# An encoder's two feed-forward layers: four form sums per layer on VectorE instead of GpSimd, and one more up chunk whose low parts a DMA makes

## The chip, the cores and the metric

The kernel runs on one core of one Trainium2 chip. The metric is device time in microseconds. Before the change the median of three runs was 1126.25 us (1124.7 to 1126.65).

## The reference

A small bidirectional encoder, batch 1, 512 tokens, width 1024, two residual layers in float32. Layer 0 mixes tokens by chunked gated linear attention, layer 1 by grouped-query attention. Each is followed by the feed-forward part that the change touches:

```python
def conv_ffn(h, w_up, w_conv, b_conv, w_down):
    u = h @ w_up                       # (512, 1024) @ (1024, 2*2816)
    u = lax.conv_general_dilated(      # depthwise, width 3, centred
        u, w_conv[:, None, :], window_strides=(1,), padding=[(1, 1)],
        dimension_numbers=('NWC', 'WIO', 'NWC'), feature_group_count=u.shape[-1]) + b_conv
    val, gate = jnp.split(u, 2, axis=-1)
    return (jax.nn.silu(gate) * val) @ w_down
...
x = x + conv_ffn(rmsnorm(x, norm_ffn[i]), ffn_w_up[i], ffn_w_conv[i], ffn_b_conv[i], ffn_w_down[i])
```

## The kernel before, in words

**High and low parts.** Every large product is made of three matmuls in a faster, less exact float format: each operand is split into a high part (the value rounded to that format) and a low part (what the rounding left). `mm3` issues high x high, high x low, low x high, so the third matmul of a product is the first that needs the weights' low part. In the names, `wh` and `wl` are the high and low parts of weights, `xhl` the two parts of the normalised input, `gu` those of the gated result, `raw` and `draw` the weights as they are loaded (up and down).

**Two kinds of up chunks.** The 5632 columns of the up matrix are taken in 22 chunks m of 128 value and 128 gate columns. The first six (`PLAIN`, m = 0 to 5) are plain: two halves (value, then gate) of 8 x 3 matmuls each over all 512 tokens into one PSUM bank `up`. The other 16 (`seven`) use a scheme of the Strassen kind with seven products of half-size blocks in place of eight; they need sums of weight blocks (`sum12`, `sum43`) and sums of blocks of the input, the *forms*. The forms are made once per layer, in `build()`, in small steps while the plain chunks run: eight `h` blocks, then the sums T1, T2, T3, T4 (tiles `ts`, line 740, by `combine`, two instructions of 128x512 for each), then a high and a low part of each form (`th`, line 734, ScalarE; `tl`, line 735, VectorE). T3 = B22 - B12 and T4 = T2 - B21 are summed on GpSimd. Chunk 6 is the first to read the forms.

**Where the low parts of the plain chunks' weights come from.** There are two ways. In `split` (lines 219 and 220) ScalarE copies the high part, rounding it, and VectorE subtracts it from `raw`. In `convert` with `by_dma` ScalarE copies the high part (line 166) and then a negative copy of `raw` into `wl` (line 168), and a DMA on GpSimd's queue adds `raw` to what is there (line 209, `accum_op=ALU.add`); the subtraction costs VectorE nothing. `BY_DMA` tells for how many plain chunks of each layer the second way is taken: 4, so chunks 0 to 3; chunks 4 and 5 are split.

**Buffers.** The parts of the weights lie in six buffers of 128x1024, that is three pairs: the next half's high copy can begin when TensorE has finished the half before the one it starts. `raw` has two buffers of a whole chunk (1 MB). A chunk's load waits until both low parts of the chunk two before it are made.

**After a plain chunk's half**: VectorE scales `up` by the token's norm into `u` (line 802), the convolution runs on ScalarE (775) and VectorE (776, 777), then silu (779), the product (780) and the split into `gu` (782, 783). Behind chunk 5 the first tiles of the down product follow (`dn`, `draw` weights, line 142 for the load, 166 and 171 for the parts), and then chunk 6 (`X`).

**What sets the order.** The functions are written in program order, but a scheduler sets each engine's order of instructions by its own costs and dependences. Each engine then works strictly in its order. An edit in one place can so move others; the change section shows where.

Of the kernel before, what the change touches and what calls it, by code (L numbers as in the profile page):

```python
# [13 lines left out]
ALU = mybir.AluOpType  # L14
# [29 lines left out]
AHEAD = 4  # L44
EARLY = 1
ROWS_AT = 3
BY_DMA = 4
FIRST_DMA = False
STEPS = 4
SHARES1 = (0, 2, 3, 3)  # L50
# [8 lines left out]
def hybrid_encoder_kernel(  # L59
# [21 lines left out]
    pe, act, dve, pool, sync = nc.tensor, nc.scalar, nc.vector, nc.gpsimd, nc.sync  # L81
# [25 lines left out]
    def big(dt, n):  # L107
        return pair("g", 22, dt, n)
# [147 lines left out]
    def add_ffn(layer):  # L256
        for m in range(PLAIN):
            W.todo.append((up[layer], m, 0))
            if m == PLAIN - 1:
                W.todo.append(("load", layer, PLAIN))  # L260
            W.todo.append((up[layer], m, 1))
            W.early += part_keys(layer, BESIDE[m])
            W.todo += part_keys(layer, BESIDE[m])
        for m in range(PLAIN, FC):
            if m + 1 < FC:
                W.todo.append(("load", layer, m + 1))
            W.todo += [(n, layer, m) for n in ("rowA1", "sum12", "sum43")]
            W.todo += part_keys(layer, BESIDE[m])
            W.todo.append(("oneA22", layer, m))
        W.todo += part_keys(layer, part_tiles(len(PARTS) - 1))  # L270
# [7 lines left out]
    add_ffn(1)  # L278
    W.by_dma += [(a, 1) for a in qk_order + [w_av]] + [(w_aout, 2)] + [(a, BY_DMA) for a in up]

# [427 lines left out]
    def ffn(layer, norm, cw, nxt):  # L708
# [4 lines left out]
        def build():  # L713

            hs = []
            for i in range(4):
                t = big(F32, "h")
                for e in range(2):
                    c = 2 * i + e
                    dve.scalar_tensor_tensor(t[:, e * S : (e + 1) * S], x[c], norm.weight(c), norm.R,  # L720
                                             ALU.mult, ALU.mult)
                    yield
                hs.append(t.rearrange("p (c s) -> p c s", s=S))
            q2 = (slice(0, 2), slice(2, 4))
            blk = lambda i, j: [hs[2 * i + q][:, :, j * H : (j + 1) * H] for q in range(2)]
            b11, b12, b21, b22 = blk(0, 0), blk(0, 1), blk(1, 0), blk(1, 1)
            v4 = lambda t: t.rearrange("p (k s) -> p k s", s=H)

            def pieces(name, srcs):
                hi, lo = v4(big(F32R, "th")), v4(big(F32R, "tl"))  # L730
                n = 4 // len(srcs)
                for q, src in enumerate(srcs):
                    sl = slice(q * n, (q + 1) * n)
                    act.activation(hi[:, sl], src, AF.Copy)
                    dve.tensor_tensor(lo[:, sl], src, hi[:, sl].bitcast(F32), ALU.subtract)
                forms[name] = (hi, lo)

            def combine(eng, dst, a, b, op):
                for q in range(2):
                    eng.tensor_tensor(dst[:, q2[q]], a[q], b[q], op)  # L740

            halves = lambda t: [t[:, q] for q in q2]
            pieces("B11", b11)
            yield
            t1, t2, t3 = (v4(big(F32, "ts")) for _ in range(3))
            combine(dve, t1, b11, b12, ALU.subtract)
            yield
            combine(dve, t2, b22, halves(t1), ALU.add)
            yield
            pieces("T2", [t2])  # L750
            yield
            pieces("T1", [t1])
            yield
            combine(pool, t3, b22, b12, ALU.subtract)
            combine(pool, t2, halves(t2), b21, ALU.subtract)
            yield
            pieces("B21", b21)
            yield
            pieces("B22", b22)
            yield  # L760
            pieces("T3", [t3])
            yield
            pieces("T4", [t2])
            yield

        building = build()

        def gated(m, u):
# [466 lines left out]
```

## Time and profile before

| | |
|---|---|
| profiled execution, time | 1126.34 us |
| its span | 1124.6 us |
| mean granted TensorE clock | 0.998 |
| TensorE, matmuls | 1104.3 us busy (98%) |
| VectorE | 887.7 us (79%) |
| ScalarE | 576.1 us (51%) |
| GpSimd | 121.2 us (11%) |
| low parts by accumulating DMA (line 209) | 32 DMAs of 512 KB, 5.3 us median from issue to landing |
| GpSimd's form sums (line 740) | 8 instructions, 20.0 us in all |
| plain chunks of layer 0 and 1 | about 232 to 300 us, about 764 to 833 us |

A row of the order of time reads: start, duration, engine, source line, operation, what is written from what, shapes, how many in a row, and in brackets how long the engine had been idle and which engine's instruction ended that. PE is TensorE, DVE VectorE, ACT ScalarE, POOL GpSimd, SP SyncE; a q behind a name is the engine's queue. Starts are microseconds from the start of the span. VectorE's and ScalarE's instructions overlap the next by some 0.1 us.

### The profile page before, as it was taken

What the parts mean: (1) busy time and instruction counts of PE and PEld (TensorE: products, weight loads), DVE (VectorE), ACT (ScalarE), POOL (GpSimd) and SP (SyncE); (2) the same over time, 40 slices, a digit from 0 to 9 for tenths busy, and PEclk for the clock granted to TensorE, in tenths of its full rate; (3) what the DMA queues carried; (4) which work ended last, traced back from release to release, by engine and by line L of the source; (5) the groups of instructions that cost most, each with busy time, mean ns of one, the idle gap of its engine ahead of it and who ended that gap; (6) DMA issues with size and microseconds to landing.
All of it is one profiled execution on the core that took longest, in us unless ns stands there. A gap on an engine that the chain in (4) does not pass through costs nothing.

```text
span 1124.6 us, 16137 instructions
## 1 busy us (share of the span) xinstructions
PE 1104.3 (98%) x6418; PEld 971.2 (86%) x6418; DVE 887.7 (79%) x1355; ACT 576.1 (51%) x854; POOL 121.2 (11%) x98
## 2 busy tenths in 40 slices
PE   9999999999899999999999999999999999999998
PEld 7878888888699999999978888888779999999996
DVE  6576654569989999979885588755997999997985
ACT  6455233465545455444474667646554545544441
POOL 0214210013000000000004333001400000000000
PEclk9999999999999999999999999999999999999999
DMA  6422220275332332323427755436433232332322
GB/s 218 142 97 76 75 75 27 97 161 128 132 112 95 112 96 93 118 73 110 168 50 195 187 159 160 140 105 159 122 131 113 95 112 83 105 113 76 113 75 75
DMA packets 30076, 128.64 MB, mean 114 GB/s; under 512 B 3505, under 2 KB 4145, under 8 KB 21297
## 3 DMA queue, kind: packets, MB, share of 16 engines
q1 hardware_dynamic: 20496, 102.30, 26.9%
q0 software_dynamic: 4608, 16.78, 7.8%
q10 hardware_dynamic: 4896, 8.54, 2.1%
q8 instruction: 50, 0.82, 0.3%
q14 instruction: 26, 0.20, 0.1%
HBM read 100.34 MB, written 2.10 MB: 91 GB/s over the span
## 4 chain that ended last, share of the span: by engine, by line
PE 78%; DVE 12%; issue 4%; ACT 3%; DMA 2%; POOL 1%; ACTq 0%; DVEq 0%; SPq 0%; POOLq 0%
PE dn L85 19%; PE Y L85 16%; PE X L85 12%; PE op L85 8%; PE vg L85 5%; PE k L85 2%; PE q L85 2%; PE up L85 2%; PE po L85 2%; PE s L85 2%; PE o L85 2%; PE A L85 1%; PE B L85 1%; DVE y L776 1%; DVE y L777 1%
## 5 line engine op out<-in xcount | busy, mean ns | idle before, releaser
L85 PE MATMUL dn<-gu,wh 128*128 128x512 f32 x708 | 219.8, 392 | 4.0 <-ACT wh L166 2.5
L85 PEld LDWEIGHTS dn<-gu,wh 128*128 128x128 f32 x708 | 130.9, 189 | 31.3 <-ACT wh L166 3.3
L85 PE MATMUL dn<-gu,wl 128*128 128x512 f32 x354 | 138.2, 391 | 1.6 <-DVE wl L171 1.6
L85 PE MATMUL up<-xhl,wh 128*128 128x512 f32 x384 | 118.8, 390 | 0.0
L775 ACT ACTIVATE y<-u,cw 128x512 f32<-128x512 f32 x88 | 68.0, 807 | 78.1 <-DVE u L875 64.1
L85 PE MATMUL X<-th,xwh 128*128 128x256 f32 x360 | 101.9, 283 | 0.0
L85 PE MATMUL X<-th,xwl 128*128 128x256 f32 x360 | 101.9, 283 | 0.0
L85 PE MATMUL X<-tl,xwh 128*128 128x256 f32 x360 | 101.9, 283 | 0.0
L166 ACT ACTIVATE wh<-raw 128x1024 fp32r<-128x1024 f32 x66 | 69.8, 1057 | 57.4 <-PE op L85 14.5
L841 DVE TENSOR_TENSOR x<-x,dn 128x512 f32<-128x512 f32 x95 | 64.7, 684 | 31.6 <-PE dn L85 31.4
L85 PEld LDWEIGHTS up<-xhl,wh 128*128 128x128 f32 x384 | 71.8, 188 | 14.8
L166 ACT ACTIVATE wh<-draw 128x1024 fp32r<-128x1024 f32 x44 | 46.7, 1061 | 71.9 <-PE dn L85 35.7
L85 PE MATMUL vg<-wh,xhl 128*128 128x512 f32 x256 | 80.3, 391 | 1.6 <-DVE wh L217 0.8
L209 POOL DMA_DIRECT2D wl<-raw x32 | 28.3, 883 | 493.1 <-ACT wl L168 487.9
L85 PEld LDWEIGHTS dn<-gu,wl 128*128 128x128 f32 x354 | 66.9, 189 | 16.0 <-DVE wl L171 2.2
L85 PE MATMUL up<-xhl,wl 128*128 128x512 f32 x192 | 75.0, 391 | 4.8 <-DVE wl L220 4.8
L85 PE MATMUL Y<-th,wh 128*128 128x256 f32 x264 | 74.7, 283 | 0.0
L85 PE MATMUL Y<-tl,wh 128*128 128x256 f32 x264 | 74.7, 283 | 0.0
L85 PE MATMUL Y<-th,wl 128*128 128x256 f32 x264 | 74.7, 283 | 0.0
L219 ACT ACTIVATE wh<-raw 128x1024 fp32r<-128x1024 f32 x40 | 42.0, 1053 | 59.9 <-PE op L85 18.8
L220 DVE TENSOR_TENSOR wl<-raw,wh 128x1024 fp32r<-128x1024 f32 x40 | 53.9, 1351 | 23.4 <-ACT wh L219 19.7
L85 PE MATMUL op<-oT,wh 128*128 128x512 f32 x256 | 71.1, 394 | 0.3 <-DVE oT L980 0.3
(232 smaller groups left out, 2872.4 us busy)
## 6 DMA issues: line engine op xcount, KB each, us to landing
raw<-in_w_up_dram SPq DMA_DIRECT2D x44, 1024.0 KB, 5.0
draw<-in_w_down_dram SPq DMA_DIRECT2D x44, 512.0 KB, 3.7
wl<-raw POOLq DMA_DIRECT2D x32, 512.0 KB, 5.3
pr<-p ACTq DMA_DIRECT2D x32, 256.0 KB, 2.5
raw<-in_w_vg_dram SPq DMA_DIRECT2D x6, 1024.0 KB, 5.0
raw<-in_w_akq_dram SPq DMA_DIRECT2D x5, 1024.0 KB, 6.2
raw<-in_w_kq_dram SPq DMA_DIRECT2D x4, 1024.0 KB, 4.8
raw<-in_w_gout_dram SPq DMA_DIRECT2D x4, 1024.0 KB, 5.1
```

The lines of the kernel that those rows point to most:

```text
L85: i = pe.matmul(*a, **k)
L166: act.activation(hi, r, AF.Copy)
L209: pool.dma_start(dst, src, accum_op=ALU.add)
L219: act.activation(hi[:, sl], r[:, sl], AF.Copy)
L220: dve.tensor_tensor(lo[:, sl], r[:, sl], hi[:, sl].bitcast(F32), ALU.subtract)
L775: act.activation(yt, ut, AF.Identity, scale=w(1), bias=w(3))
L776: dve.scalar_tensor_tensor(yt[:, 1:], ut[:, : S - 1], w(0), yt[:, 1:], ALU.mult, ALU.add)
L777: dve.scalar_tensor_tensor(yt[:, : S - 1], ut[:, 1:], w(2), yt[:, : S - 1], ALU.mult, ALU.add)
L841: dve.tensor_tensor(x[c], x[c], ps, ALU.add)
```

## The change

The two sums T3 and T4 go to VectorE, and `BY_DMA` becomes 5, so that chunk 4's weights get their low parts by DMA too, in both layers.

```diff
-BY_DMA = 4
+BY_DMA = 5
...
-            combine(pool, t3, b22, b12, ALU.subtract)
-            combine(pool, t2, halves(t2), b21, ALU.subtract)
+            combine(dve, t3, b22, b12, ALU.subtract)
+            combine(dve, t2, halves(t2), b21, ALU.subtract)
```

In the order of instructions this shows as follows. In layer 0, `raw_2149` is chunk 4's weights (`wh_2151`, `wl_2152` its first half), `raw_2232` (then `raw_2234`) chunk 5's; `ts_2072` to `ts_2074` are the form sums. GpSimd, before and after, from chunk 3's accumulates on:

```order
L209 DMA wl_2038<-raw_2035 128x1024
L209 DMA wl_2086<-raw_2035 128x1024
L740 TENSOR_TENSOR ts_2074<-h_2014,h_1977 128x512
L740 TENSOR_TENSOR ts_2074<-h_2017,h_1980 128x512
L740 TENSOR_TENSOR ts_2073<-ts_2073,h_2014 128x512
L740 TENSOR_TENSOR ts_2073<-ts_2073,h_2017 128x512
```
```order
L209 DMA wl_2038<-raw_2035 128x1024
L209 DMA wl_2086<-raw_2035 128x1024
L209 DMA wl_2152<-raw_2149 128x1024
L209 DMA wl_2191<-raw_2149 128x1024
L209 DMA wl_5032<-raw_5029 128x1024
```

The four sums have left the queue, and two accumulates of chunk 4 stand in their place. ScalarE, layer 0, from the high copy of chunk 4's first half on, before and after:

```order
L219 ACTIVATE wh_2151<-raw_2149 128x1024
L734 ACTIVATE th_2079<-ts_2073 128x1024
L775 ACTIVATE y_2135<-u_2033,cw 128x512
L734 ACTIVATE th_2114<-ts_2072 128x1024
L734 ACTIVATE th_2122<-h_2014 128x512
L734 ACTIVATE th_2122<-h_2017 128x512
L734 ACTIVATE th_2128<-h_2014 128x512
L734 ACTIVATE th_2128<-h_2017 128x512
L219 ACTIVATE wh_2189<-raw_2149 128x1024
```
```order
L166 ACTIVATE wh_2151<-raw_2149 128x1024
L734 ACTIVATE th_2079<-ts_2073 128x1024
L775 ACTIVATE y_2135<-u_2033,cw 128x512
L734 ACTIVATE th_2114<-ts_2072 128x1024
L168 ACTIVATE wl_2152<-raw_2149 128x1024
L734 ACTIVATE th_2122<-h_2014 128x512
L734 ACTIVATE th_2122<-h_2017 128x512
L166 ACTIVATE wh_2190<-raw_2149 128x1024
L168 ACTIVATE wl_2191<-raw_2149 128x1024
L734 ACTIVATE th_2128<-h_2014 128x512
L734 ACTIVATE th_2128<-h_2017 128x512
```

The negative copy of the first half (line 168) stands three instructions behind its high copy, and the second half's two copies have moved up between the form copies. In layer 1 the first half's negative copy stands directly behind its high copy. VectorE, layer 0, from the subtraction of chunk 4's first half on, before, and the same place after:

```order
L220 TENSOR_TENSOR wl_2152<-raw_2149,wh_2151 128x1024
L735 TENSOR_TENSOR tl_2080<-ts_2073,th_2079 128x1024
L735 TENSOR_TENSOR tl_2115<-ts_2072,th_2114 128x1024
L735 TENSOR_TENSOR tl_2123<-h_2014,th_2122 128x512
L735 TENSOR_TENSOR tl_2123<-h_2017,th_2122 128x512
```
```order
L735 TENSOR_TENSOR tl_2115<-ts_2072,th_2114 128x1024
L740 TENSOR_TENSOR ts_2074<-h_2014,h_1977 128x512
L740 TENSOR_TENSOR ts_2074<-h_2017,h_1980 128x512
L740 TENSOR_TENSOR ts_2073<-ts_2073,h_2014 128x512
L740 TENSOR_TENSOR ts_2073<-ts_2073,h_2017 128x512
L735 TENSOR_TENSOR tl_2123<-h_2014,th_2122 128x512
```

The subtraction is gone, and the four sums stand between the low parts of T1 and of B21. Some rows further down, the subtraction for chunk 5's first half stands ahead of the low parts of T3 and T4, where it stood behind them before.

## The prediction

> **What bounds the kernel now.** I read the page first, then TensorE's waits, then its order of time around each wait, and last VectorE (DVE), GpSimd (POOL), ScalarE (ACT) and the DMAs beside the longest ones.
>
> ```profile
> PE 1104.3 (98%) x6418; PEld 971.2 (86%) x6418; DVE 887.7 (79%) x1355; ACT 576.1 (51%) x854; POOL 121.2 (11%) x98
> ```
>
> TensorE is busy for 98% of the span, and the change takes no matmul away. All that can be won is idle time of TensorE, so its waits come next (engine, line and what it waited for: us in total, times, longest).
>
> ```profile
> PE up L85 <- DVE wl L220: 4.8, 2, 2.7
> PE dn L85 <- ACT wh L166: 2.5, 2, 1.8
> PE dn L85 <- DVE wl L171: 1.6, 1, 1.6
> PE X L85 <- ACT wh L166: 0.8, 1, 0.8
> ```
>
> These four rows are 9.7 us, and all of it lies in the plain chunks of the two FFN layers and directly behind them. Two are for low parts that VectorE makes (L220, L171). TensorE's order of time tells where (start, duration, then in brackets the idle time before and who ended it):
>
> ```profile
> 276.10 0.39 PE L85 MATMUL up<-xhl,wl 128*128 128x512 f32 x1
> ...
> 286.54 0.61 PE L85 MATMUL up<-xhl,wh 128*128 128x512 f32 x2
> 289.26 0.50 PE L85 MATMUL up<-xhl,wl 128*128 128x512 f32 x1 [2.10 <-DVE wl L220]
> ...
> 300.66 0.96 PE L85 MATMUL dn<-gu,wh 128*128 128x512 f32 x3 [0.66 <-ACT wh L166]
> 303.21 0.50 PE L85 MATMUL dn<-gu,wl 128*128 128x512 f32 x1 [1.59 <-DVE wl L171]
> ```
> ```profile
> 808.16 0.61 PE L85 MATMUL up<-xhl,wh 128*128 128x512 f32 x2
> 811.46 0.50 PE L85 MATMUL up<-xhl,wl 128*128 128x512 f32 x1 [2.69 <-DVE wl L220]
> ...
> 834.87 1.20 PE L85 MATMUL dn<-gu,wh 128*128 128x512 f32 x4 [1.81 <-ACT wh L166]
> ```
>
> A half of a chunk is 24 matmuls, and its third is the first that needs the low part. 276.10 is the third matmul of chunk 4's first half, 286.54 the first of chunk 5's: 46 matmuls in 10.44 us, 0.227 each. A matmul's modelled duration (0.39) overlaps the next one, so a bracket understates what is lost; I count start against due start. Chunk 5's third matmul was due at 286.54 + 2 x 0.227 = 286.99 and came at 289.26. Without any wait the down tile would start at 286.54 + 48 x 0.227 = 297.44, and its fourth matmul (first low part) at 298.12; it came at 303.21. So layer 0 loses 5.1 us here. In layer 1 chunk 4's third matmul was due at 808.16 + 0.45 = 808.61 and came at 811.46: 2.85 lost, and 1.8 more ahead of the down tile.
>
> Why is VectorE late? Line 740 is the sums of the input's forms, 776 and 777 the convolution:
>
> ```profile
> 262.86 4.42 DVE L740 TENSOR_TENSOR ts<-h 128x512 f32<-128x512 f32 x2
> 267.20 1.28 DVE L740 TENSOR_TENSOR ts<-h,ts 128x512 f32<-128x512 f32 x2
> ...
> 269.01 0.73 DVE L776 SCALAR_TENSOR_TENSOR y<-u,cw,y 128x511 f32<-128x511 f32 x1
> 269.67 1.21 DVE L220 TENSOR_TENSOR wl<-raw,wh 128x1024 fp32r<-128x1024 f32 x1
> ...
> 275.48 1.78 DVE L776 SCALAR_TENSOR_TENSOR y<-u,cw,y 128x511 f32<-128x511 f32 x1
> 277.18 2.43 DVE L777 SCALAR_TENSOR_TENSOR y<-u,cw,y 128x511 f32<-128x511 f32 x2
> ```
> ```profile
> 809.13 2.28 DVE L220 TENSOR_TENSOR wl<-raw,wh 128x1024 fp32r<-128x1024 f32 x1
> ```
> ```profile
> 263.86 2.86 POOL L740 TENSOR_TENSOR ts<-h,h 128x512 f32<-128x512 f32 x2
> 272.16 6.25 POOL L740 TENSOR_TENSOR ts<-ts,h 128x512 f32<-128x512 f32 x2 [5.44 <-DVE tl L735]
> ```
> ```profile
> 801.68 6.97 POOL L740 TENSOR_TENSOR ts<-ts,h 128x512 f32<-128x512 f32 x2 [6.19 <-DVE tl L735]
> 808.61 3.94 POOL L740 TENSOR_TENSOR ts<-h,h 128x512 f32<-128x512 f32 x2
> ```
>
> Just while GpSimd runs its sums, VectorE's instructions are stretched: two sums took 4.42 in place of 1.28, three convolution steps 1.78 + 2.43 = 4.21 in place of 3 x 0.73 = 2.19, and in layer 1 the very subtraction for which TensorE waits took 2.28 in place of 1.21. GpSimd holds VectorE up for 3.14 + 2.02 = 5.2 us in layer 0.
>
> **The change, part by part.** *Sums to VectorE.* Per layer VectorE gets four sums of 0.64 (1.28 for two), +2.6 us, and no longer stands beside GpSimd: -5.2 in layer 0. GpSimd loses its sums; nobody waited for them on TensorE's path.
>
> *Chunk 4's low parts by DMA.* VectorE loses two subtractions of 1.21: -2.4 per layer. So its line in layer 0 gets ahead by 5.2 + 2.4 - 2.6 = 5.0 us. ScalarE gets two negative copies, and GpSimd's queue two accumulating DMAs. ScalarE is strictly in order, so what counts is when each copy comes:
>
> ```profile
> 261.96 1.04 ACT L168 ACTIVATE wl<-raw 128x1024 fp32r<-128x1024 f32 x1
> ...
> 264.70 1.06 ACT L219 ACTIVATE wh<-raw 128x1024 fp32r<-128x1024 f32 x1 [0.98 <-PE up L85]
> 268.58 1.06 ACT L734 ACTIVATE th<-ts 128x1024 fp32r<-128x1024 f32 x1 [2.82 <-DVE ts L740]
> ...
> 271.20 2.18 ACT L734 ACTIVATE th<-h 128x512 fp32r<-128x512 f32 x4
> ```
> ```profile
> 797.25 1.07 ACT L219 ACTIVATE wh<-raw 128x1024 fp32r<-128x1024 f32 x1 [0.64 <-PE up L85]
> ```
> ```profile
> 263.30 0.86 POOL L209 DMA_DIRECT2D wl<-raw  x1 [6.32 <-ACT wl L168]
> ```
> ```profile
> L147 SPq DMA_DIRECT2D raw<-in_w_up_dram x1: 328/328/328, 268.3 to 268.3; - x1
> DMA to landing us min/median/max: 4.9/4.9/4.9
> ```
> ```profile
> L147 SPq DMA_DIRECT2D raw<-in_w_up_dram x1: 328/328/328, 776.7 to 776.7; - x1
> ...
> L209 POOL DMA_DIRECT2D wl<-raw x1: 862/862/862, 777.8 to 777.8; - x1
> DMA to landing us min/median/max: 6.5/6.5/6.5
> ```
> ```profile
> L147 SPq DMA_DIRECT2D raw<-in_w_up_dram x1: 327/327/327, 799.4 to 799.4; - x1
> ```
> ```profile
> DMA to landing us min/median/max: 4.5/5.3/9.2
> ```
>
> Layer 0, first half: the high copy stays at 264.70 (TensorE frees its buffer then) and ends about 265.7. The T2 sum is done by 262.86 + 4 x 0.64 = 265.4 instead of 268.5, so ScalarE's next three instructions (two form copies and a y between them, 268.58 to 271.20, 2.62 us) run 265.7 to 268.3. Then the negative copy to 269.3, and 0.3 later (261.96 + 1.04 = 263.00 to 263.30) the DMA at 269.6. Chunk 5's load is then 1.3 us under way; an accumulate issued 1.1 behind a load took 6.5. It lands at 276.1, and TensorE needs it at 276.10: no wait, or a few tenths. The ends over all 32 accumulates are 4.5 (slack 2.0) and 9.2 (2.7 late); I take 6.5, the like case.
>
> Layer 1, first half: high copy 797.25, negative copy right behind, DMA at about 799.5 together with chunk 5's load; even at the longest, 9.2, it lands at 808.7 and is due at 808.61. No wait, against 2.85 before. The second halves are due 24 x 0.227 = 5.4 us later, and their copies start when TensorE begins chunk 3's second half, 5.4 us behind the first's slot, with two form copies between high and low part at most: 2 us of slack.
>
> *What follows in layer 0.* Chunk 5's first low part was 2.27 late and VectorE's line is 5.0 ahead, with the subtraction moved ahead of two form pieces too: gone. The down tile's low part must come 5.1 earlier than before, and the line is ahead by 5.0: the wait shrinks to 0 to 0.3. Its high part on ScalarE was late behind a y that waited for VectorE, so that goes too. Gain 5.1 (4.8 to 5.1).
>
> *What follows in layer 1.* The wait ahead of the down tile stays:
>
> ```profile
> 828.33 1.28 SPq L142 DMA_DIRECT2D draw<-in_w_down_dram  x3
> ```
> ```profile
> 833.76 1.06 ACT L166 ACTIVATE wh<-draw 128x1024 fp32r<-128x1024 f32 x1 [1.65 <-DMA draw<-in_w_down_dram]
> ```
>
> The draw that ScalarE waits for is the second of three on SyncE's queue, behind one whose buffer TensorE frees in chunk 5's second half. That is a time on TensorE's own line, so load and need move together: 1.8 stays. Of the 0.8 for X I give 0.25 back (0 to 0.8), because the y ahead of its high part on ScalarE no longer waits for VectorE. Gain 2.85 + 0.25 = 3.1.
>
> The sum: 5.1 + 3.1 = 8.2. The profiled execution took 1126.34 (0.09 above the median of the runs shown), so 1118.1. What hides the added work: ScalarE's four copies and the four DMAs fill idle time (ScalarE is busy 51%); if that cover failed the price would be the lateness of the DMA above.
>
> [...]
>
> **The rivals.** *The half-speed stretch goes too.* After the idle stretch in layer 1 the granted clock dropped (busy of PE, PEld, DVE, ACT, POOL, then PEclk, DMA share and GB/s):
>
> ```profile
> 837.00:841.00 4.00, 4.00 (x11) 3.09 (x12) 3.24 (x4) 0.78 (x1) 0.00 (x0) 0.57 0.00 0
> ```
>
> At 0.57 of the clock these 4 us do the work of 2.3, so 1.7 are lost. If the shorter stretch of waits after the change (1.8 and 0.55 in place of 1.8 and 0.8) does not set it off, the time is 1118.1 - 1.7 = 1116.4. Against it: most of the idle time is still there. [...]
>
> *The accumulate is late.* In layer 0 it lands up to 9.2 behind its issue, 2.7 late, and gain shrinks to 5.5: 1120.8, or 1122.5 if the new wait costs a half-speed stretch. It decides from a landing above 6.5.
>
> *Slower.* The same mechanism, at chunk 4's first half in both layers: a landing of 11.9 is 5.4 late in layer 0 and 2.8 in layer 1, together the 8.2 gained; beyond that the kernel is slower (14 us: 7.5 + 4.9 - 8.2 = 4.2, 1130.5). Against it: 9.2 is the longest of 32.
>
> *VectorE gains nothing.* If something else than GpSimd stretched its rows, its balance is +2.6 - 2.4 = +0.2 and layer 0 keeps its waits; layer 1 still loses the wait for line 220: 1126.3 - 2.85 + 0.2 = 1123.7. Against it: the stretched rows and GpSimd's sums coincide in both layers.
>
> **How the numbers follow.** Forecast (waits gone, half-speed stretch stays) 0.50, at 1118.1; stretch gone too 0.25, at 1116.4; late accumulate 0.14, at 1120.8 to 1122.5; VectorE gains nothing 0.06, at 1123.7; slower 0.04; other 0.01. A range of 1115.9 to 1122.6 holds the first three, 0.89, which leaves something for terms mis-sized by a microsecond. 0.2%, about what a measurement here can tell from no change, is 2.25 us, so faster means below 1124.0: the first three and half of the fourth, 0.92, which I lower to 0.88; same 0.08; slower 0.04.
>
> **What would show it.** Right: no stretched row on VectorE at line 740, 776 or 220; no wait of TensorE for line 220, and those for the down tile's weights gone in layer 0, with about 1.8 left in layer 1; accumulates of chunk 4 landing before about 276.1 and 808.6. Wrong: a wait of TensorE for DMA wl<-raw at chunk 4, a negative copy on ScalarE that waits for VectorE's form sums, or VectorE still back to back and late at the first down tile.

## The result

The changed kernel takes 1117.78 us in the median (1117.27 to 1118.27), the kernel before in the same rounds 1126.45; the ratio is 0.9926, with a 95% interval of 0.9909 to 0.9943. Forecast were 1118.1 us, between 1115.9 and 1122.6. The profiled execution took 1117.27 with a span of 1115.5.

The page's first part and TensorE's waits, after:

```profile
PE 1103.2 (99%) x6418; PEld 971.6 (87%) x6418; DVE 878.6 (79%) x1359; ACT 579.9 (52%) x858; POOL 103.7 (9%) x94
```
```profile
PE dn L85 <- ACT wh L166: 1.7, 1, 1.7
...
PE X L85 <- ACT wh L166: 0.5, 1, 0.5
```

Of the four waiting rows of before, the two for low parts by VectorE (L220, L171) are gone. The row for the down tile's high part is down from two waits to one, the one in layer 1. TensorE's order of time after, first around layer 0's chunk 5 and down tile, then layer 1's chunk 4 and down tile:

```profile
286.54 0.62 PE L85 MATMUL up<-xhl,wh 128*128 128x512 f32 x2
287.00 0.39 PE L85 MATMUL up<-xhl,wl 128*128 128x512 f32 x1
...
297.42 1.07 PE L85 MATMUL dn<-gu,wh 128*128 128x512 f32 x4
298.33 0.48 PE L85 MATMUL dn<-gu,wl 128*128 128x512 f32 x1
```
```profile
803.14 0.50 PE L85 MATMUL up<-xhl,wl 128*128 128x512 f32 x1
...
826.46 1.20 PE L85 MATMUL dn<-gu,wh 128*128 128x512 f32 x4 [1.70 <-ACT wh L166]
828.11 0.58 PE L85 MATMUL X<-th,wh 128*128 128x256 f32 x1 [0.46 <-ACT wh L166]
```

In layer 0 no bracket is left: chunk 5's third matmul comes at 287.00 (before 289.26) and the down tile starts at 297.42 (before 300.66). In layer 1 chunk 4's third matmul comes without a bracket; the wait ahead of the down tile is still there. VectorE (DVE) after, layer 0, and the issues on GpSimd (POOL):

```profile
262.92 1.29 DVE L740 TENSOR_TENSOR ts<-h 128x512 f32<-128x512 f32 x2
264.12 1.29 DVE L740 TENSOR_TENSOR ts<-h,ts 128x512 f32<-128x512 f32 x2
...
270.30 1.29 DVE L740 TENSOR_TENSOR ts<-h,h 128x512 f32<-128x512 f32 x2
271.50 1.29 DVE L740 TENSOR_TENSOR ts<-ts,h 128x512 f32<-128x512 f32 x2
...
275.12 0.74 DVE L777 SCALAR_TENSOR_TENSOR y<-u,cw,y 128x511 f32<-128x511 f32 x1
...
276.98 1.21 DVE L220 TENSOR_TENSOR wl<-raw,wh 128x1024 fp32r<-128x1024 f32 x1
...
278.71 1.40 DVE L776 SCALAR_TENSOR_TENSOR y<-u,cw,y 128x511 f32<-128x511 f32 x2
```
```profile
269.66 0.85 POOL L209 DMA_DIRECT2D wl<-raw  x1 [5.45 <-ACT wl L168]
272.60 0.86 POOL L209 DMA_DIRECT2D wl<-raw  x1 [2.09 <-ACT wl L168]
```
```profile
DMA to landing us min/median/max: 5.6/5.8/6.1
```

The pair that took 4.42 takes 1.29, the two pairs that GpSimd made in 2.86 and 6.25 take 1.29 each, convolution steps (lines 776 and 777) take 0.7 each where they took up to 1.8, and chunk 5's first low part, made from 287.99 before, is made from 276.98. The last row is for chunk 4's two accumulates in layer 0.

To see where time comes from in each kernel below, I take the start of the same matmul (by its count on TensorE) in a trace and in the trace of before, and show by how much the difference changes over each stretch (negative: gained, us). What traces lose or win ahead of 16 us is left out; more on it at the end. A row tells of one traced run: for the sums alone and for GpSimd subtracting that run was the slowest of its kernel (1128.58 and 1128.09 us, 3.0 and 2.7 above the medians given below).

| kernel | layer 0 chunk 4 | chunk 5 | down tile | up to layer 1 | layer 1 chunks 4, 5 | down tile, X | sum |
|---|---|---|---|---|---|---|---|
| after | 0.0 | -2.4 | -2.7 | -0.5 | -2.6 | -0.7 | -9.1 |
| sums only | 0.1 | -2.4 | +2.8 | +0.7 | -0.9 | 0.0 | +0.2 |
| DMA part only | +6.2 | -2.4 | -2.8 | -0.3 | +1.3 | -4.9 | -3.0 |
| before, draws in order | 0.0 | 0.0 | 0.0 | +0.1 | 0.0 | -2.5 | -2.5 |
| sums only, draws in order | 0.0 | -2.4 | -0.6 | -0.5 | +0.8 | -3.0 | -5.8 |
| after, draws in order | 0.0 | -2.4 | -2.7 | +0.2 | -3.0 | -3.5 | -11.5 |
| after, chunk 5 by DMA too | 0.0 | -2.4 | -0.7 | -0.3 | -2.5 | -4.6 | -10.5 |
| after, GpSimd subtracting | +1.1 | -2.4 | +1.6 | +0.2 | +1.8 | -0.9 | +1.3 |
| after, GpSimd filling | 0.0 | -2.4 | -2.7 | -0.5 | -2.2 | -2.0 | -9.8 |

### The profile page after: what moved, and what is told of

It is laid out like the page before. It is cut to its first block, busy times and chain, and to the rows that moved or that the text cites. A ratio compares the mean times of both kernels' runs of the same rounds, so it can differ in the third digit from the quotient of the medians.

```text
span 1115.5 us, 16152 instructions
## 1 busy us (share of the span) xinstructions
PE 1103.2 (99%) x6418; PEld 971.6 (87%) x6418; DVE 878.6 (79%) x1359; ACT 579.9 (52%) x858; POOL 103.7 (9%) x94
## 4 chain that ended last, share of the span: by engine, by line
PE 88%; DVE 4%; DMA 3%; issue 2%; ACT 2%; POOL 1%; ACTq 0%; SPq 0%; DVEq 0%; POOLq 0%
PE dn L85 20%; PE Y L85 16%; PE X L85 12%; PE up L85 8%; PE op L85 8%; PE vg L85 5%; PE B L85 2%; PE A L85 2%; PE k L85 2%; PE q L85 2%; PE po L85 2%; PE s L85 2%; PE o L85 2%; DMA wl<-raw 1%; PE av L85 1%
## 5 line engine op out<-in xcount | busy, mean ns | idle before, releaser
L209 POOL DMA_DIRECT2D wl<-raw x36 | 31.6, 878 | 509.9 <-ACT wl L168 509.8
L85 PEld LDWEIGHTS X<-th,xwh 128*128 128x128 f32 x360 | 69.0, 192 | 0.8 <-DVE v L855 0.7
```

What stands on the lines that cost most here:

```text
L85: i = pe.matmul(*a, **k)
L209: pool.dma_start(dst, src, accum_op=ALU.add)
```

## The experiments

The theory: GpSimd's sums stretched VectorE, so moving them speeds VectorE up although it gets more to do; the DMA part takes the subtraction out from under layer 1's wait. Rivals: one of the parts does it alone; VectorE's stretch has another cause.

**Only the sums.** `BY_DMA = 4` in the changed kernel.

> Only the sums move to VectorE; chunk 4's low parts stay subtractions on VectorE (line 220). Theory (GpSimd's sums hold VectorE up): VectorE's line in layer 0 gets 5.2 us back, takes the four sums (2.6) and keeps its two subtractions, so it is 2.6 ahead: chunk 5's low part (2.27 late before) is in time, the first down tile's, which must come 5.1 earlier, is still 2.5 late, a gain of 2.6. In layer 1 the subtraction for chunk 4 stands behind the sums: old end of the T2 piece 803.31 + sums 2.57 + four form pieces 2.49 + two convolution steps 1.40 + itself 1.21 = 810.98 in place of 811.41, a gain of 0.4. Together 3.0, 1123.3 us. Rival (VectorE's stretched rows have another cause than GpSimd): VectorE only gets 2.6 more work per layer ahead of late low parts, and the time rises to about 1126.3 + 2 x 2.6 = 1131.5. No line 740, 776 or 220 row should be over 1.3 us a pair by the theory; 2 to 4.4 by the rival.

Measured: 1125.54 us, ratio to before 0.9992 (0.9982 to 1.0002), no change. VectorE's rows came as the theory has them (pairs of 1.28 to 1.29), and chunk 5's wait went, 2.4 us. But the 2.4 was given back at layer 0's down tile. TensorE's row there, ScalarE's, and SyncE's issues of draws:

```profile
303.46 2.08 PE L85 MATMUL dn<-gu,wh 128*128 128x512 f32 x4 [3.75 <-ACT wh L166]
```
```profile
302.35 1.06 ACT L166 ACTIVATE wh<-draw 128x1024 fp32r<-128x1024 f32 x1 [3.86 <-DMA draw<-in_w_down_dram]
```
```profile
290.83 0.33 SPq L179 DMA_DIRECT2D raw<-in_w_up_dram  x1
294.98 1.81 SPq L142 DMA_DIRECT2D draw<-in_w_down_dram  x3
```

The draw that the first down tile needs was compiled into second place of the three on SyncE's queue (it landed at 302.33, the one ahead of it at 299.69), behind one whose buffer TensorE frees only in chunk 5, as it stands in layer 1 of the kernels before and after. In layer 0 of those it goes out first, right behind the raw load. So this run changed two things, and neither theory nor rival had said so: the order of the draws is a side effect of the compiled order, worth several us. The next runs hold it fixed.

**Only the DMA part.** `BY_DMA = 5` in the kernel before; the sums stay on GpSimd.

> Only chunk 4's low parts move to accumulating DMAs; the sums stay on GpSimd. By the plain sum of the two parts (the theory that they are independent) it gains VectorE's two subtractions, 2.4 us in layer 0, and the 2.85 of the wait for line 220 in layer 1: 1126.3 - 5.3 = 1121.0. The rival, which I hold likelier: the issues stand behind the sums on GpSimd's own queue. In layer 0 both sums pairs come ahead of the first issue; they start when T2's low piece is done (about 267) and take 10 to 11 beside VectorE, so the issue comes at about 278 and lands near 283.5, due 276.10: 7.4 late, in place of the 5.1 lost there before. In layer 1 the first half's issue is ahead of the sums and in time, the second half's behind them: issue about 812.7, landing 818, due 814.1: 4 late in place of 2.85. Together 3.5 slower than before, 1129.8 us; the waits of TensorE are for the DMA into wl and none for line 220 of chunk 4.

Measured: 1123.44 us, ratio 0.9969 (0.9957 to 0.998). Neither number came, but the rival's mechanism did, in GpSimd's queue and on TensorE in layer 0:

```profile
271.06 3.90 POOL L740 TENSOR_TENSOR ts<-ts,h 128x512 f32<-128x512 f32 x2 [4.53 <-DVE tl L735]
274.93 3.43 POOL L740 TENSOR_TENSOR ts<-h,h 128x512 f32<-128x512 f32 x2
278.31 1.77 POOL L209 DMA_DIRECT2D wl<-raw  x2
```
```profile
282.93 0.50 PE L85 MATMUL up<-xhl,wl 128*128 128x512 f32 x1 [4.31 <-DMA wl<-raw]
```

Both accumulates stand behind 7.3 us of sums; chunk 4 loses 6.2 us in layer 0 (7.4 expected) and chunks 4 and 5 lose 1.3 in layer 1 (1.2 expected). The 6.2 only covers what layer 0 lost later anyway (5.2). What I had not foreseen is 4.9 won at layer 1's down tile: here the needed draw had been compiled into first place.

**The draws in order.** The changed kernel, with the other draws tied behind the early one, which the first down tile needs, on SyncE (nothing else by hand):

```diff
-                sync.dma_start(t, src[i][:, h * 2 * S : (h + 1) * 2 * S])
+                with tc.issue_after(self.drawn.ins) if self.drawn and key not in self.early else ExitStack():
+                    i_ = sync.dma_start(t, src[i][:, h * 2 * S : (h + 1) * 2 * S])
+                self.drawn = i_ if key in self.early else self.drawn
```

> The changed kernel, with the first down tile's draw kept ahead of the next draws on SyncE's queue in layer 1 (order only; layer 0 has this order already). Theory (the wait that stayed ahead of layer 1's down tile, 1.70 us, is the queue's order alone): the draw goes out right behind the raw load at 814.65, lands about 820.5 in place of 825.33, ScalarE has its high part before TensorE needs it at 824.76, and 1.70 goes. If the 0.46 for X's weights still comes but no half-speed stretch follows (1.7), the time is 1117.8 - 1.7 - 1.7 = 1114.4; if the stretch stays although the long wait is gone, 1116.1. Rival (the draw's own buffer is freed late too): it waits on SyncE, with the other two draws now behind it, and the time is 1117.8 or up to 2 more.

Measured: 1115.29 us (1114.85 to 1115.7), ratio to before 0.99 (0.9886 to 0.9913). SyncE's first draw goes out at 816.27, right behind the raw load at 815.84; TensorE, and the rows by stretch (busy of PE, PEld, DVE, ACT, POOL, then PEclk, DMA share, GB/s) of this kernel, then of the changed one:

```profile
825.41 1.07 PE L85 MATMUL dn<-gu,wh 128*128 128x512 f32 x4
827.59 0.50 PE L85 MATMUL dn<-gu,wl 128*128 128x512 f32 x1 [1.10 <-DVE wl L173]
```
```profile
828.00:832.00 4.00, 4.00 (x19) 3.31 (x18) 4.00 (x5) 0.20 (x1) 0.00 (x0) 1.00 0.00 0
```
```profile
828.00:832.00 4.00, 3.89 (x12) 3.17 (x13) 3.15 (x4) 1.01 (x2) 0.00 (x0) 0.59 0.00 0
```

The wait for the high part is gone and so is the half-speed stretch (PEclk 1.00 against 0.59); 1.10 comes back for the draw's low part on VectorE. The theory had 1114.4, without this wait; the measured time is 0.9 above it.

**The same order in the kernel before and with the sums alone** (the same edit in each):

> The kernel before, with the first down tile's draw kept ahead of the next two on SyncE's queue (in layer 0 it is so already; in layer 1 it stood second). Theory (what the draws' order costs has nothing to do with the change): the wait ahead of layer 1's down tile (1.8), the one at X (0.8) and the half-speed stretch behind them (1.7) go, 4.3 in all, with up to 1 given back for the draw's low part on VectorE: 1126.4 - 3.8 = 1122.6 (1121.9 to 1123.6). Layer 0 is as before. Rival (in the kernel before VectorE is so late that the draw's order does not decide): 1126.4 within 1.

> Only the sums on VectorE, as in the run of the sums alone, with the draws' order kept in both layers. That run gained 2.42 at layer 0's chunk 5 and gave it back at the down tile, where the needed draw had slipped to second place on SyncE's queue; in layer 1 it gained 0.85 at chunk 4. Theory (the slip is a side effect of the compiled order, not of the sums): with the order kept the 2.42 stays, the down tile's low part comes 1 to 2.7 earlier than before as VectorE's line is 3.2 ahead there, and layer 1 gains 0.85 and some 3.6 for its draw: 1126.4 - 2.4 - 1.5 - 0.85 - 3.6 = 1118.0 (1116.8 to 1119.5). Rival (VectorE's extra 2.6 us of sums eat the gain): layer 0 gains nothing and the time is that of the kernel before with the order kept, about 1122.5.

Measured: 1124.65 us (ratio 0.9986, 0.9976 to 0.9996) and 1121.54 (0.9955, 0.9941 to 0.9969). Both gained less than the theory had, and the first lies between its theory and its rival. VectorE is late at the down tiles there: in the kernel before with the draws in order, layer 1's down tile waits 2.12 for its low part, where up to 1 was allowed. TensorE with the sums alone:

```profile
300.43 0.50 PE L85 MATMUL dn<-gu,wl 128*128 128x512 f32 x1 [1.97 <-DVE wl L173]
...
807.11 0.50 PE L85 MATMUL up<-xhl,wh 128*128 128x512 f32 x1 [1.82 <-ACT wh L221]
```

The first row: layer 0's down tile still waits 2.0 for its low part (5.14 - 2.97 = 2.2 short of what the changed kernel gains; my first estimate, made for the sums alone, was 2.5). The second: in layer 1 the sums push a convolution back on VectorE, ScalarE's next y waits for it, the high copy of chunk 4's second half stands behind that y, and TensorE's compiled order has one matmul of that half ahead of the first half's low part. With the draws in order the four kernels, by medians, are (the DMA part alone needed no tie, its needed draw goes out first in both layers):

| | low parts of chunk 4 by VectorE | by DMA |
|---|---|---|
| sums on GpSimd | 1124.65 | 1123.44 |
| sums on VectorE | 1121.54 | 1115.29 |

The parts are not independent: 3.1 and 1.2 apart, 9.4 together. The rows of the table were timed in different rounds; each against the kernel before in its own rounds, the steps are 3.1, 0.9 and 9.1. About 1 us for the DMA part is no more than single runs differ by, but the gap between 4 and 9 is well beyond that. Without the DMA part VectorE is about 2.2 short at layer 0's down tile; without the move of the sums the accumulates stand behind them.

**GpSimd made to work again.** The changed kernel with four useless subtractions per layer on GpSimd, released by a copy of 8 columns behind the T2 sum; then the same with memsets in their place:

```diff
+            dve.tensor_copy(junk[:, :8], t2[:, 0, :8])
...
+                    pool.tensor_tensor(junk, x_[q], y_[q], ALU.subtract)
```
```diff
+                pool.memset(junk, 0.0)
```

> The changed kernel with four useless subtractions of 128x512 per layer added on GpSimd, released by VectorE's T2 sum (through a copy of 8 columns), so that they run where the sums ran before; VectorE's own order is the changed one. Theory (GpSimd's two-input instructions hold VectorE's two-input instructions up, whatever they compute): VectorE's rows of lines 735, 740, 776/777 beside them are stretched again, by about 5 us in layer 0 (3.14 + 2.02 before), and chunk 4's first accumulate, behind them on GpSimd's queue, is issued 4 to 8 us later than 269.66 and lands 3 to 7 late: the time 1117.8 + 5 = 1123 (1120 to 1126). Rival (the sums' data or buffers, not GpSimd's running, stretched VectorE): VectorE's rows stay at 0.64 to 0.74 an instruction, GpSimd needs 4 x 1.4 = 5.7 us, and only the accumulate costs something, 1 to 3 us.

> As the run with the useless subtractions, but the four instructions on GpSimd are memsets of the same 128x512: they write and read nothing. Theory 1 (any instruction of GpSimd holds VectorE up): VectorE's rows beside them are stretched as beside subtractions, by as much as GpSimd is busy. Theory 2 (only a GpSimd instruction that reads does): all rows of VectorE stay at 0.64 to 0.74 an instruction, chunk 4's accumulate is issued at most 1 to 2 us later, and the time is that of the changed kernel, 1117.8 within 1.5. [...]

Measured: 1125.42 us with the subtractions (ratio 0.9992, 0.9983 to 1.0002), 1118.08 with the memsets (0.9923, 0.9908 to 0.9938). GpSimd and VectorE in layer 0, with the subtractions:

```profile
265.94 6.94 POOL L759 TENSOR_TENSOR junk<-h,h 128x512 f32<-128x512 f32 x4 [1.37 <-DVE junk L755]
```
```profile
265.76 0.69 DVE L808 TENSOR_TENSOR u<-up,R 128x512 f32<-128x512 f32 x1
266.37 1.42 DVE L782 SCALAR_TENSOR_TENSOR y<-u,cw,y 128x511 f32<-128x511 f32 x1
267.82 1.67 DVE L783 SCALAR_TENSOR_TENSOR y<-u,cw,y 128x511 f32<-128x511 f32 x1
269.42 2.31 DVE L735 TENSOR_TENSOR tl<-ts,th 128x1024 fp32r<-128x1024 f32 x1
271.65 1.79 DVE L782 SCALAR_TENSOR_TENSOR y<-u,cw,y 128x511 f32<-128x511 f32 x1
```

and with the memsets:

```profile
267.22 2.28 POOL L758 MEMSET junk<- 128x512 f32 x4 [1.33 <-DVE junk L755]
```
```profile
267.67 0.74 DVE L781 SCALAR_TENSOR_TENSOR y<-u,cw,y 128x511 f32<-128x511 f32 x1
268.44 0.75 DVE L782 SCALAR_TENSOR_TENSOR y<-u,cw,y 128x511 f32<-128x511 f32 x1
269.11 1.22 DVE L735 TENSOR_TENSOR tl<-ts,th 128x1024 fp32r<-128x1024 f32 x1
270.24 0.75 DVE L781 SCALAR_TENSOR_TENSOR y<-u,cw,y 128x511 f32<-128x511 f32 x1
```

The same four VectorE instructions take 7.19 beside subtractions and 3.46 beside or just after memsets. The sums' results and their buffers have nothing to do with it: subtractions that nobody reads do the same. The gain is gone with them, part of it through chunk 4's accumulates, which stand behind them on GpSimd's queue (+1.1 at chunk 4 of layer 0), the rest through VectorE: TensorE again waits for low parts that VectorE makes, 1.4 at layer 0's down tile and 2.0 at line 220 in layer 1, and half-speed stretches follow (mean granted clock 0.995, in the changed kernel 0.998). Writing alone does not do it, so theory 2 is the one that fits; an instruction of GpSimd that reads one tile was not tried, and the memsets were also shorter (0.53 each). The first row of the VectorE fence, 0.69, is an instruction with one input in PSUM (`up`), not stretched although GpSimd was at work from 265.94 on.

**One more chunk by DMA.** `BY_DMA = 6`.

> The changed kernel with chunk 5's low parts by accumulating DMA as well. Theory (VectorE's lateness is gone already, and TensorE waits for no low part of a plain chunk any more): VectorE gets another 2.4 us per layer free that nobody waits for, so no change, 1117.8 within 1. Rival (VectorE's subtractions still cost something in the plain chunks): up to 1 to 2 us faster. Against both: the raw load behind it on SyncE's queue now waits for the accumulate's landing, 5 to 6 us behind the copy, in place of a subtraction of 1.2; the first draw stands behind that load and had 2.7 us to spare in layer 0, so up to 2 us slower if it comes over 3 us later.

Measured: 1117.1 us, ratio to before 0.9914 (0.9901 to 0.9928): no change against the changed kernel, as expected, but as a sum of two effects. The row of the table has 2.0 less gained at layer 0's down tile, and 3.9 more at layer 1's, where the needed draw again happened to be compiled first. The former is the price named for it:

```profile
300.16 1.06 ACT L166 ACTIVATE wh<-draw 128x1024 fp32r<-128x1024 f32 x1 [2.37 <-DMA draw<-in_w_down_dram]
```

The draw goes out at 292.78 behind a raw load that waited for the accumulate; TensorE then waits 1.09 for this copy.

**A version that is faster than both.** The kernel with the draws in order again, with the changed kernel beside it, and one in which the low parts for the chunks of seven products are tied behind the draw's low part on VectorE (in the text below, the seventh products' low parts):

> The changed kernel itself, on the same chip as the two beside it: 1117.8 within 1, so that the gain of keeping the draws' order (2.5 by the medians so far) is seen against it in the same rounds. By the traces so far TensorE's clock stays low for a time at the start that differs from run to run (first full-speed mark at 4.35 to 10.8 us), which makes single times differ by up to 2.6 us.

> The changed kernel with the draws' order kept, again, beside the changed kernel: 1115.3 within 1. If its gain of 2.5 was only the chip or the start of that run, it is at 1117.8.

> The changed kernel with the draws' order kept, and with the draw's low part put ahead of the seventh products' low parts on VectorE. Theory (the 1.10 us that TensorE still waits at layer 1's first down tile is VectorE taking another low part and a copy first, 825.11 to 826.31): the 1.10 goes, 1115.3 - 1.1 = 1114.2. Rival (the instructions that it passes, and TensorE's products that the compiled order moves with them, are needed as early): the wait comes back at the X products behind, and the time is 1115.3 or up to 1.5 more.

Measured in the same rounds: 1117.48 us (ratio to before 0.992, 0.9908 to 0.9933) for the changed kernel, 1115.78 (0.9906, 0.9893 to 0.992) with the draws in order, 1115.03 (0.9896, 0.9881 to 0.9911) with the low parts tied too. The order of the draws gained 1.7 here and 2.5 in the first comparison. Tying the low parts shows no gain beyond the spread: VectorE spends the time ahead of the draw's low part waiting for TensorE's last `up` bank instead,

```profile
825.83 0.69 DVE L806 TENSOR_TENSOR u<-up,R 128x512 f32<-128x512 f32 x1 [0.42 <-PE up L85]
826.44 1.22 DVE L174 TENSOR_TENSOR wl<-draw,wh 128x1024 fp32r<-128x1024 f32 x1
```

and TensorE's wait of 1.10 becomes 1.01.

## Why the prediction was right, step by step

*GpSimd stretches VectorE (5.2 us in layer 0).* Right, and shown from both sides: the rows are unstretched without GpSimd's sums, and stretched by 3.7 again beside 6.9 us of useless subtractions. Not every row beside the sums was stretched in the kernel before: four low parts of `h` blocks (line 735, from 273.07) took 2.48 with a pair of GpSimd's sums running from 272.16 to 278.41, and 2.49 in the changed kernel without.

*Layer 0, 5.1.* Measured 2.42 + 2.72 = 5.14 from chunk 4 to the down tile: the matmul that started at 303.21 before starts at 298.10 by count. The compiled order has put one more high part ahead of the first low part there, which comes at 298.33, without a wait. VectorE's line, forecast 5.0 ahead, has the draw's low part at 297.04 in place of 301.93, 4.9. The gain was 2.4 at chunk 5 and 2.7 at the down tile.

*Chunk 4's accumulate in layer 0: issued at 269.6, landing at 276.1.* Issued at 269.66, landed 6.1 later at 275.7, due 276.12. In layer 1 I took no wait even at the longest landing, 9.2. It took 9.2:

```profile
DMA to landing us min/median/max: 5.3/7.3/9.2
```

It landed at 803.10, and the matmul came 0.2 late. That is most of the difference between 2.85 and the measured 2.6. In four later traces (the changed kernel again, the draws in order again, the low parts tied too, the memsets) this wait was 0.2 to 0.5. So the term was not nothing, but small.

*Layer 1's down tile: 1.8 stays, X gives 0.25.* 1.70 stayed, and X's wait went from 0.80 to 0.46. The stretch gained 0.7, 0.45 of it from these two waits; the half-speed time, which stayed as forecast, cost a little less, since its first 0.2 us (827.90 to 828.11) fell into the wait for X. That it stayed was partly luck: the kernel with the memsets had nearly the same two waits, 1.87 and 0.47, and kept full speed (the last section shows where they fell). But the reason I gave, that load and need move together, holds only for the compiled order of the draws: with the needed draw first the wait goes. I had read the order as given, from the kernel before. The same slip in layer 0 cost the kernel with the sums alone 3.4 us (+2.8 against -0.6 in the table), and the prediction had no rival for it. In the changed kernel layer 0's draw is compiled first, which is why the sum came out: that was luck, since nothing in the prediction says what the change does to SyncE's order.

*The sum.* 8.2 forecast, 8.7 by medians, 9.1 between the profiled spans. The 0.5 between the layers was in no term; in the second trace of the changed kernel that stretch lost 0.2, so it belongs to single runs.

*The issues on GpSimd.* The issue at 263.30 took 0.86 in the kernel before, with VectorE's sum running beside it, and the forecast allowed for no delay by VectorE. Chunk 4's issues took 0.85 and 0.86 with VectorE back to back, and the first came 0.3 behind ScalarE's copy, as forecast.

*Rivals.* The accumulate was not late in layer 0. That VectorE gains nothing is refuted by its rows. The half-speed stretch did not go with X's shorter wait. With the draws in order it went when the wait of 1.70 did, and in the memsets' kernel it did not come, where the wait of 1.87 fell across a boundary (1.45 and 0.42, in the last section).

## What to carry to other kernels

Look for VectorE instructions that run long, and at what GpSimd does meanwhile (here four took 7.19 us beside GpSimd's subtractions, 3.46 beside or just after its memsets): giving VectorE the work can be cheaper than sharing it. Before two edits are added up, see which queue each puts behind which: here an accumulating DMA was worth little (about 1 us) until GpSimd's queue had no arithmetic left ahead of it. And compare the order of each DMA queue before and after any edit, since a load that slips one place can take all that the edit wins (with the sums alone 2.8 us lost at layer 0's down tile, 2.4 won at chunk 5).

## What the hardware showed that I had not expected

In all eleven half-speed stretches of these traces the half-speed time (0.50 in the marks of the granted clock in the trace) is 3.41 us long and begins on a grid of 3.413 us, counted from the trace's first full-speed mark: in the changed kernel 827.90 - 5.29 = 822.61 = 241.0 x 3.413, in the kernel before 837.20 - 4.35 = 832.85 = 244.0 x 3.413. In these traces the stretches went with TensorE's idle time inside one window of that grid, not with a wait's length. The kernel before waited 2.69 at chunk 4 of layer 1 across a boundary (809.90, so 1.12 and 1.57) and kept full speed there. The memsets' kernel waited 1.87, longer than the changed kernel's 1.70, but across a boundary (828.46, so 1.45 and 0.42), and kept full speed; the sums alone, draws in order, waited 1.82 inside one window and lost it:

```profile
828.00:832.00 4.00, 2.65 (x11) 1.96 (x12) 3.95 (x5) 3.44 (x4) 0.00 (x0) 1.00 0.02 8
```
```profile
808.00:812.00 4.00, 4.00 (x12) 3.11 (x11) 4.00 (x6) 4.00 (x6) 0.00 (x0) 0.57 0.37 92
```

Summed by window, the idle time of TensorE ahead of a half-speed stretch was 1.90 (before), 1.94 (after), 2.14 and 3.41 (sums only), 1.97 and 2.57 (DMA part only), 1.90 and 2.14 (GpSimd subtracting). Windows with 1.73 or less idle (the 1.73 in the DMA part alone) were never followed by one, once the clock was up and until the kernel's last microseconds. Between 1.77 and 1.82 three windows were (1.77, 1.79, 1.82) and one was not (1.82, the kernel before with the draws in order); ends of matmuls are modelled, so a tenth is not certain. Why the clock keeps such a grid, the traces do not show.

The first full-speed mark itself comes at 4.35 to 10.8 us. Rows of 4 us from the start, the changed kernel, then the sums alone:

```profile
8.00:12.00 4.00, 4.00 (x20) 3.30 (x19) 4.00 (x8) 4.00 (x8) 0.00 (x0) 1.00 1.01 358
```
```profile
8.00:12.00 4.00, 4.00 (x15) 3.22 (x14) 4.00 (x8) 4.00 (x8) 0.00 (x0) 1.00 1.01 361
```

15 matmuls against 20 in the same 4 us (the granted clock is not marked there). The traces with a late mark are up to 2.6 us behind at 16 us and stay so; single runs of one kernel differ by about that much and more (1.0 us in the changed kernel's first runs, 6.0 with the sums alone), which is why differences of 1 us between medians are not read here.
